# Row factors behind the second value pair, opening loads in pieces, and low parts on GpSimd, in a streaming hybrid layer on one core

## The chip, the core and the metric

The kernel runs on one core of a Trainium2 chip. A core has five engines that work side by side, each on its own queue of instructions, in order: TensorE (PE in the profile; PEld is its weight load) for matrix products, VectorE (DVE) and ScalarE (ACT) for elementwise work, GpSimd (POOL) for some more of that, and SyncE (SP), which here only issues transfers. Data lie in DRAM, in the on-chip SBUF (128 partitions) and in PSUM, the banks that TensorE writes to. Engines wait for each other by semaphores. The metric is the device time of one execution, in microseconds (us); a lower one is better.

## What is computed

The reference is one layer of a streaming encoder for 512 prompt frames and 64 frames of a running stream (576 in all, 2048 channels, fp32). The part that matters here is its beginning:

```python
hn = rmsnorm(x, g_norm1)
proj = hn @ w_in
q, k, v, gb, gc, hc = jnp.split(proj, [...], axis=-1)
q = rmsnorm(q.reshape(B, T, N_HEADS, HEAD_DIM), g_q)
k = rmsnorm(k.reshape(B, T, N_HEADS, HEAD_DIM), g_k)
v = v.reshape(B, T, N_HEADS, HEAD_DIM)
...
x = x + mix @ w_out
h2 = rmsnorm(x, g_norm2)
x = x + (jax.nn.silu(h2 @ w_gate) * (h2 @ w_up)) @ w_down
```

Attention (stick breaking), a short gated convolution and the output norms stand between; the change touches none of them.

## The kernel before

Activations are held with channels on the partitions and the 576 frames along the row, in two halves of 288. A product in fp32 is made of three products in a shorter format: a tensor is split into a high part (a cast) and a low part (tensor minus high part), and high x high, low x high and high x low are summed in PSUM. `split` (L230) does this: the cast on ScalarE, the subtraction on VectorE. Larger products then use a seven-product scheme on 2x2 blocks, which needs sums of blocks of the activations (b11, b12, bod and the sums t12a, t34a) and of the weights.

The row factor of the first norm, 1/sqrt(mean of squares), is not put on x. It is applied to the results, as a row vector R1 copied to all partitions.

The first 80 us of the kernel are one stage (L618 to L752). Its order on ScalarE, VectorE and SyncE is written by hand (`manual_schedule`), TensorE's is for the whole kernel; GpSimd's, and that of all engines but TensorE behind the stage, is left to the framework. It has two loops over the 16 blocks of 128 input channels (kt):

- The first loop turns x and computes the first value pair (heads 0 and 1). `turn_x(kt)` (L541) transposes a block of x on TensorE (four transposes for the prompt, and every fourth block four small ones for the sample frames), copies it out on ScalarE (st), scales it by the norm's gains g1c and splits it: the even blocks give b11 and b12 with the high part on ScalarE, the odd ones give bod, both parts on VectorE. `step0(0, ..., kt)` (L661) makes the 12 products of a block, LAG = 3 turns later. `split_wv` (L630) splits a quarter of the pair's weights, 1024 columns, into whi and wlo. Behind the loop the result goes to the tiles E0.
- The second loop computes the second value pair (heads 2 and 3) from the same blocks, `step0(1, ..., kt)`. Beside it ScalarE and VectorE sum the squares of x (`x_squares`, L604: three rows on ScalarE, the fourth on VectorE) and make the block sums for what follows: `x_sums(j)` (L573) computes, for a pair j of blocks, two scaled copies on ScalarE (b11s, b22s), t1 and t3 on VectorE, t2 = b22s - t1 on GpSimd and t4, which needs t2, on VectorE; `x_parts(j)` (L591) splits them into t12a and t34a. Pairs 0 to 2 are done in the first loop, 3 to 7 in the second.

In turn 9 of the second loop the squares are reduced, GpSimd takes the power (L730), VectorE puts the factors on the diagonal of `dg` (L737, turn 11), and in turn 13 TensorE transposes a block of vectors (`turn_vectors`) and multiplies `dg` by ones into PSUM (L743), from which VectorE copies R1. So turns 13 to 15 of the second pair stand behind these products in TensorE's queue.

Behind the stage the second pair is scaled by R1 (e1, L899), the first as well (e0, L904, on VectorE); `tokens` turns and stores them a number of TensorE's steps later. Then units of the projection follow in the list `order`: `run(n, p)` makes the p-th of seven products of a unit, `prepare(n, p)` splits its weights four places ahead; two of these splits, of the first unit, stand in the second loop already.

Loads and stores are issued by SyncE. The opening order (L636 to L653) is x, sample rows, gains, x, the first quarter of the value weights in one piece, x, and so on.

Of the kernel before, what the change touches and what calls it, by code (L numbers as in the profile page):

```python
# [16 lines left out]
P = 128  # L17
# [84 lines left out]
def tile_hybrid_stream_step(  # L102
# [405 lines left out]
    t12a, t34a = {}, {}  # L508

# [31 lines left out]
    def turn_x(kt):  # L541
        j, q = divmod(kt, 2)
        c = next(c for c, (k0, k1) in enumerate(XCH) if k0 <= kt < k1)
        k = kt - XCH[c][0]
        if kt % 8 == 0:
            banks["s"] = misc("psx_s")
# [4 lines left out]
        psx = ps_z.tile([P, 512], F32, tag=f"z{kt % 2}", name=f"psx{kt}")  # L551
        for i in range(4):
            nc.tensor.transpose(psx[:, i * P : (i + 1) * P], xin[c][:, i, k * P : (k + 1) * P], ident)
# [19 lines left out]
    def x_sums(j, tag):  # L573
# [7 lines left out]
        ta, tb = (tmp.tile([P, 2, HALF], F32, tag=tag, name="tab", bufs=3 if tag == "hl" else 2) for _ in range(2))  # L581
# [4 lines left out]
        nc.vector.scalar_tensor_tensor(out=t4, in0=od[:, :HALF], scalar=go, in1=t2, op0=ALU.mult, op1=ALU.subtract)  # L586
        tabs[j] = ta, tb

    tabs = {}

    def x_parts(j):  # L591
        ta, tb = tabs.pop(j)
# [25 lines left out]
    LAG = 3  # L618
    with tc.manual_schedule(engines={mybir.EngineType.Activation, mybir.EngineType.DVE, mybir.EngineType.SP}):
# [5 lines left out]
        def load_wv(v, q):  # L625
            c0 = 2 * AW + 2 * v * P
            nc.sync.dma_start(out=raw0(q).rearrange("p (k c) -> p k c", k=4),
                              in_=w_in[4 * q * P : 4 * (q + 1) * P, c0 : c0 + 2 * P].rearrange("(k p) c -> p k c", p=P))

        def split_wv(v, q):  # L630
            if q % 2 == 0:
                wv[v, q // 2] = [wpool.tile([P, 2048], F32R, tag=tag, name=tag) for tag in ("whi", "wlo")]
            hi, lo = (t[:, q % 2 * 1024 : (q % 2 + 1) * 1024] for t in wv[v, q // 2])
            split(hi, lo, raw0(q))

        load_x(0)  # L636
        load_s(0)
        nc.sync.dma_start(out=g1raw, in_=g_norm1[0].rearrange("(r c) -> r c", c=P))
        load_x(1)
        load_wv(0, 0)  # L640
# [32 lines left out]
        for kt in range(KD + LAG):  # L673
            if kt < KD:
                if kt == 0:
                    psg = misc("ps_g1")
                    nc.tensor.transpose(psg[:, :KD], g1raw, ident[:KD, :KD])
                    nc.vector.tensor_copy(out=g1c, in_=psg[:, :KD])
                turn_x(kt)
            if kt in (0, 4, 8, 12):  # L680
# [13 lines left out]
            if kt in (13, 15):  # L694
# [911 lines left out]
```

## Time and profile before

| | us |
|---|---|
| median of three runs | 2406.14 (2406.02 to 2406.74) |
| the profiled execution, its own time | 2408.49 |
| its span in the profile | 2406.8 |
| first value pair, from its first product to the second pair's | 12.13 to 46.05 |
| second value pair, up to the first product of the first unit | 46.05 to 80.31 |

The profile is of one execution. A row of a timeline gives the start, the duration, the engine, the line of the kernel, the operation, the tile written and the tiles read, the shape and the number of instructions; in brackets stands how long the engine had been idle before and what ended that. A row of the stretches gives for each engine the busy time and the number of instructions (PE, PEld, DVE, ACT, POOL), then the clock granted to TensorE (1.00 is full speed), the share of the transfer engines and GB/s. Consecutive rows of one engine can overlap slightly: what an instruction costs its queue is the distance from its start to the next one's.

### The profile page before, as it was taken

The page shows a single profiled execution, that of the slowest core. Times are in us where ns is not written, and L with a number is a line of the kernel's source. Part 1 is how long each engine was busy: PE and PEld are TensorE (multiplying, and loading weights), DVE is VectorE, ACT ScalarE, POOL GpSimd, SP SyncE. Part 2 cuts the span into 40 slices and gives each one's busy share as a digit, 9 for nine tenths or more (in the row PEclk, how much of TensorE's full clock was granted, in tenths as well). Part 3 has the DMA queues.
Part 4 walks back from the last instruction along what each step waited for, and adds up shares of the span by engine and source line. Part 5 has one row for each costly group of instructions (what it writes and reads, how often), then busy time and mean ns, then how long its engine had stood idle before and what let it go on. Part 6 is the DMA issues. An engine that isn't in the chain of part 4 may idle for free.

```text
span 2406.8 us, 43812 instructions
## 1 busy us (share of the span) xinstructions
PE 2355.5 (98%) x17609; PEld 2339.5 (97%) x17609; DVE 1939.7 (81%) x2840; ACT 1235.0 (51%) x2207; POOL 298.9 (12%) x377
## 2 busy tenths in 40 slices
PE   8899999999999999999999999999999899999998
PEld 8899999998889999999999999999999899999998
DVE  7888898797677768888888888888888778887875
ACT  7456656455677545444444444444444444444454
POOL 0111121120233222000000000000000002431211
PEclk9999999999999999999999999999999999999999
DMA  7433342535632233535444444444444936885642
GB/s 253 140 113 108 108 140 86 161 99 184 224 107 89 100 127 118 155 112 158 150 128 145 146 143 132 144 150 141 129 152 141 339 112 205 221 226 195 205 128 79
DMA packets 474900, 360.60 MB, mean 150 GB/s; under 512 B 11278, under 2 KB 460680, under 8 KB 474696
## 3 DMA queue, kind: packets, MB, share of 16 engines
q1 hardware_dynamic: 469528, 351.02, 45.7%
q0 software_dynamic: 5168, 6.79, 1.6%
q8 instruction: 138, 2.26, 0.4%
q14 instruction: 66, 0.54, 0.1%
HBM read 281.39 MB, written 76.37 MB: 149 GB/s over the span
## 4 chain that ended last, share of the span: by engine, by line
PE 82%; DVE 6%; ACT 4%; issue 2%; POOL 2%; DMA 1%; SPq 0%; ACTq 0%; DVEq 0%; POOLq 0%
PE psy L405 43%; PE psw L405 21%; PE psx L405 10%; PE pjo L227 5%; DVE whl L232 1%; ACT whl L231 1%; PE pw L1388 1%; ACT ph L231 0%; PE psv L405 0%; PE pot L1511 0%; DVE c L866 0%; DVE raw_b L349 0%; POOL hbl L1117 0%; DMA raw_a<-in_w_down_dram 0%; DVE wlo L180 0%
## 5 line engine op out<-in xcount | busy, mean ns | idle before, releaser
L232 DVE TENSOR_TENSOR whl<-raw_a,whl 128x1024 fp32r<-128x1024 f32 (+4 forms) x376 | 426.4, 1135 | 69.4 <-ACT whl L231 67.8
L405 PE MATMUL psy<-t,whl 128*128 128x288 f32 x2916 | 438.4, 295 | 0.5 <-ACT part L428 0.5
L231 ACT CAST whl<-raw_a 128x1024 fp32r<-128x1024 f32 (+4 forms) x376 | 352.6, 938 | 137.9 <-PE psx L405 47.8
L405 PE MATMUL psy<-h_s,whl 128*128 128x288 f32 x2724 | 411.7, 295 | 6.8 <-ACT part L428 6.8
L405 PEld LDWEIGHTS psy<-t,whl 128*128 128x128 f32 x2916 | 403.7, 189 | 0.9 <-ACT part L428 0.7
L405 PEld LDWEIGHTS psy<-h_s,whl 128*128 128x128 f32 x2724 | 378.5, 189 | 7.3 <-ACT part L428 7.3
L405 PE MATMUL psw<-t,whl 128*128 128x288 f32 x2592 | 377.1, 295 | 0.0
L405 PEld LDWEIGHTS psw<-t,whl 128*128 128x128 f32 x2592 | 354.4, 189 | 0.2
L232 DVE TENSOR_TENSOR whl<-raw_b,whl 128x1024 fp32r<-128x1024 f32 (+5 forms) x230 | 248.7, 1081 | 86.4 <-ACT whl L231 85.1
L231 ACT CAST whl<-raw_b 128x1024 fp32r<-128x1024 f32 (+5 forms) x230 | 207.6, 904 | 206.9 <-PE psw L405 70.8
L428 ACT COPY part<-psy 128x288 f32<-128x288 f32 x303 | 121.2, 400 | 348.5 <-PE psy L405 346.4
L405 PE MATMUL psx<-h_s,whl 128*128 128x288 f32 x1122 | 165.1, 295 | 2.7 <-DVE gs L1368 2.7
L405 PEld LDWEIGHTS psx<-h_s,whl 128*128 128x128 f32 x1122 | 154.1, 188 | 2.9 <-issue 2.9
L231 ACT CAST whl<-s 128x1024 fp32r<-128x1024 f32 (+5 forms) x101 | 93.4, 924 | 119.9 <-PE psw L405 112.3
L405 PE MATMUL psy<-t12a,whl 128*128 128x288 f32 x1056 | 150.5, 295 | 3.1 <-ACT part L428 3.1
L405 PE MATMUL psw<-t34a,whl 128*128 128x288 f32 x1056 | 150.4, 295 | 2.1 <-DVE ghs L854 0.9
L405 PEld LDWEIGHTS psy<-t12a,whl 128*128 128x128 f32 x1056 | 143.5, 188 | 4.0 <-ACT part L428 4.0
L405 PEld LDWEIGHTS psw<-t34a,whl 128*128 128x128 f32 x1056 | 143.2, 188 | 2.7 <-DVE ghs L854 1.1
L227 PE MATMUL pjo<-mixc,whi 128*128 128x288 f32 x512 | 123.0, 307 | 1.2 <-ACT kcT L1063 1.2
L232 DVE TENSOR_TENSOR whl<-s,whl 128x1024 fp32r<-128x1024 f32 (+5 forms) x101 | 107.5, 1064 | 19.6 <-ACT whl L231 18.0
L1331 POOL DMA_DIRECT2D hid_dram<-form x3 | 2.4, 809 | 921.1 <-DVE form L232 921.1
L227 PE MATMUL pjo<-mixa,whi 128*128 128x288 f32 x512 | 102.1, 295 | 0.0
(599 smaller groups left out, 4146.8 us busy)
## 6 DMA issues: line engine op xcount, KB each, us to landing
hid_dram<-form SPq DMA_DIRECT2D x147, 288.0 KB, 2.3
raw_a<-in_w_gate_dram SPq DMA_DIRECT2D x23, 1024.0 KB, 6.2
raw_a<-in_w_up_dram SPq DMA_DIRECT2D x23, 1024.0 KB, 5.5
raw_a<-in_w_in_dram SPq DMA_DIRECT2D x22, 1024.0 KB, 5.5
raw_b<-in_w_in_dram SPq DMA_DIRECT2D x22, 1024.0 KB, 7.9
raw_b<-in_w_gate_dram SPq DMA_DIRECT2D x21, 1024.0 KB, 6.6
raw_b<-in_w_up_dram SPq DMA_DIRECT2D x21, 1024.0 KB, 7.7
h_s<-hid_dram SPq DMA_DIRECT2D x10, 2016.0 KB, 9.2
```

The source lines that it names most:

```text
L227: mm(ps, w_[:, k, csl], x_[:, a:b], start=(k == 0 and n == 0), stop=(k == nk - 1 and n == 2))
L231: nc.scalar.copy(out=hi, in_=src)
L232: (lo_eng or nc.vector).tensor_tensor(out=lo, in0=src, in1=hi.bitcast(F32), op=ALU.subtract)
L405: mm(ps, whl[:, w_, j, :], x_, start=(start and j == 0 and q == 0), stop=(j == len(xs_) - 1 and q == 2), skip_group_check=True)
L428: nc.scalar.copy(out=t, in_=st["y"])
L1331: q.dma_start(out=hid_dram[fp][2 * n - 2 : 2 * n].rearrange("f p t -> p f t"), in_=t.bitcast(F32))
L1388: mm(pss[j, i], w_[:, k, j * P : (j + 1) * P], x_, start=(kk == 0 and k == 0 and n == 0), stop=(kk == 1 and k == 7 and n == 2))
```

## The change

It has these parts:

- `step0(0, ..., 0)` runs in turn 1, and LAG is 2 for the others. The block of x is transposed ahead of the sample rows and of the gains.
- The first quarter of the value weights is loaded and split in two halves; the first half is split by VectorE alone, at the head of its queue. The first sample rows and the gains are loaded by ScalarE's queue.
- The low parts of the four quarters of the second pair's weights are computed on GpSimd, the first two of them two turns earlier (turns 11 and 13 of the first loop), the others in turns 0 and 3 of the second loop. The scaling of e0 by R1 goes to GpSimd as well.
- t4 is moved from `x_sums` to the beginning of `x_parts` (`x_last`). In the second loop `x_parts(j - 1)` stands right behind `x_sums(j)`, and `x_parts(7)` behind the loop. The fourth row of squares of pairs 5 to 7 goes to ScalarE.
- The reduction of the squares moves to turn 11 and `dg` to turn 13; the products with ones, the copies of R1 and `turn_vectors` stand behind the 16 turns of the second pair. They use one full bank and part of a second, and the second pair's banks are z1, z2 and two shared ones in place of z0, z1 and two shared ones.
- The tokens of the value heads are turned some steps later.

```diff
-    def load_s(c):
+    def load_s(c, queue=nc.sync):
...
-        nc.sync.dma_start(out=xsn[c], in_=xs[:, 4 * c * P : 4 * (c + 1) * P])
+        queue.dma_start(out=xsn[c], in_=xs[:, 4 * c * P : 4 * (c + 1) * P])
...
-    def x_sums(j, tag):
+    def x_sums(j, tags):
...
         nc.vector.scalar_tensor_tensor(out=t1, in0=ev[:, HALF:], scalar=ge, in1=b11s, op0=ALU.mult, op1=ALU.subtract)
         nc.gpsimd.tensor_tensor(out=t2, in0=b22s, in1=t1, op=ALU.subtract)
         nc.vector.scalar_tensor_tensor(out=t3, in0=ev[:, HALF:], scalar=ge, in1=b22s, op0=ALU.mult, op1=ALU.subtract)
-        nc.vector.scalar_tensor_tensor(out=t4, in0=od[:, :HALF], scalar=go, in1=t2, op0=ALU.mult, op1=ALU.subtract)
         tabs[j] = ta, tb
+    def x_last(j):
+        (ta, tb), od, go = tabs[j], stp[j][:, 1], g1c[:, 2 * j + 1 : 2 * j + 2]
+        nc.vector.scalar_tensor_tensor(out=tb[:, 1], in0=od[:, :HALF], scalar=go, in1=ta[:, 1], op0=ALU.mult,
+                                       op1=ALU.subtract)
...
     def x_parts(j):
+        x_last(j)
         ta, tb = tabs.pop(j)
...
-    def x_squares(j):
+    def x_squares(j, eng=nc.scalar):
...
-                square(xin[c][:, i, :], ssx[:, i, c : c + 1], nc.vector if i == 3 else nc.scalar)
+                square(xin[c][:, i, :], ssx[:, i, c : c + 1], eng if i == 3 else nc.scalar)
...
-    LAG = 3
+    LAG = 2
...
+            if v == q == a == 0:
+                nc.vector.tensor_copy(hi, raw0(q)[:, a:b])
+                nc.vector.tensor_tensor(out=lo, in0=raw0(q)[:, a:b], in1=hi.bitcast(F32), op=ALU.subtract)
+            else:
+                split(hi, lo, raw0(q)[:, a:b], lo_eng)
...
         load_x(0)
-        load_s(0)
-        nc.sync.dma_start(out=g1raw, in_=g_norm1[0].rearrange("(r c) -> r c", c=P))
+        load_s(0, nc.scalar)
+        nc.scalar.dma_start(out=g1raw, in_=g_norm1[0].rearrange("(r c) -> r c", c=P))
+        load_wv(0, 0, 0, 2)
         load_x(1)
-        load_wv(0, 0)
+        load_wv(0, 0, 2, 4)
         load_x(2)
...
+                    split_wv(0, 0, 0, 2)
                 turn_x(kt)
-            if kt in (0, 4, 8, 12):
+                if kt == 1:
+                    split_wv(0, 0, 2, 4)
+                    step0(0, v0ps, 0)
+            if kt in (4, 8, 12):
                 split_wv(0, kt // 4)
...
-            if kt in (13, 15):
-                split_wv(1, (kt - 13) // 2)
+            if kt in (11, 13):
+                split_wv(1, (kt - 11) // 2, lo_eng=nc.gpsimd)
...
-            if kt >= LAG:
+            if LAG < kt:
                 step0(0, v0ps, kt - LAG)
...
-            if kt in (1, 4):
-                split_wv(1, 2 + kt // 4)
-            if kt in (0, 2, 4, 6, 8):
-                x_squares(3 + kt // 2)
+            if kt in (0, 3):
+                split_wv(1, 2 + kt // 3, lo_eng=nc.gpsimd)
+            if kt in (0, 2, 5, 8, 10):
+                j = {0: 3, 2: 4, 5: 5, 8: 6, 10: 7}[kt]
+                x_squares(j, nc.vector if j < 5 else nc.scalar)
...
-            if kt == 9:
+            if kt == 11:
                 nc.vector.reduce_sum(out=ssr, in_=ssx, axis=mybir.AxisListType.X)
...
-            if kt in (1, 4, 7, 10, 13):
-                x_sums(3 + (kt - 1) // 3, "hl")
+            if kt in (1, 4, 7, 9, 12):
+                j = {1: 3, 4: 4, 7: 5, 9: 6, 12: 7}[kt]
+                x_sums(j, ("hl", "hl" if j % 2 else "c1"))
+                if j > 3:
+                    x_parts(j - 1)
             if kt == 10:
                 prepare(-NA, 1)
-            if kt == 15:
+            if kt == 13:
+                dg = lpool.tile([P, UW - 2], F32, tag="c0", name="dg")[:, :T]
+                for i, (o, n) in enumerate(row_pieces()):
+                    nc.vector.tensor_scalar(out=dg[:n, o : o + n], in0=ident[:n, :n], scalar1=rst[:n, i : i + 1],
+                                            scalar2=None, op0=ALU.mult)
                 prepare(-NA, 2)
             step0(1, v1ps, kt)
+        psr, psv = (ps_pj.tile([P, 512], F32, tag="pj", name=name) for name in ("ps_r1", "ps_vec"))
+        for i, (o, n) in enumerate(row_pieces()):
+            mm(psr[:, o : o + n] if i < 4 else psv[:, P : P + n], oner.bitcast(F32)[:n, :], dg[:n, o : o + n],
+               start=True, stop=True)
+        nc.vector.tensor_copy(R1[:, :TP], psr)
+        nc.vector.tensor_copy(R1[:, TP:], psv[:, P : P + TS])
+        turn_vectors(psv)
...
-        pipe.spawn(tokens(e1[c], vp[:, 2 + c, :], vs[:, 2 + c, :], v_dram[2 + c], 4 + 5 * c))
+        pipe.spawn(tokens(e1[c], vp[:, 2 + c, :], vs[:, 2 + c, :], v_dram[2 + c], 9 + 5 * c))
...
-        nc.vector.tensor_tensor(out=e0[c], in0=e0[c], in1=R1, op=ALU.mult)
-        pipe.spawn(tokens(e0[c], vp[:, c, :], vs[:, c, :], v_dram[c], 24 + 8 * c))
+        nc.gpsimd.tensor_tensor(out=e0[c], in0=e0[c], in1=R1, op=ALU.mult)
+        pipe.spawn(tokens(e0[c], vp[:, c, :], vs[:, c, :], v_dram[c], 30 + 8 * c))
...
         prepare(*order[k_])
+    x_parts(7)
```

More of the change, by code (lines that the diff above doesn't have):

```diff
@@ L508, in tile_hybrid_stream_step @@
     t12a, t34a = {}, {}
+    UW = T + 4
     def a_frame(p_, j):
@@ L544, in turn_x @@
         k = kt - XCH[c][0]
+        psx = ps_z.tile([P, 512], F32, tag=f"z{kt % 2}", name=f"psx{kt}")
+        for i in range(4):
+            nc.tensor.transpose(psx[:, i * P : (i + 1) * P], xin[c][:, i, k * P : (k + 1) * P], ident)
         if kt % 8 == 0:
@@ L550, in turn_x @@
                 nc.tensor.transpose(banks["s"][:, o : o + TS], xsn[kt // 4][:, s * P : (s + 1) * P], ident[:TS, :TS])
-        psx = ps_z.tile([P, 512], F32, tag=f"z{kt % 2}", name=f"psx{kt}")
-        for i in range(4):
-            nc.tensor.transpose(psx[:, i * P : (i + 1) * P], xin[c][:, i, k * P : (k + 1) * P], ident)
+        if kt == 0:
+            psg = misc("ps_g1")
+            nc.tensor.transpose(psg[:, :KD], g1raw, ident[:KD, :KD])
+            nc.vector.tensor_copy(out=g1c, in_=psg[:, :KD])
         if q == 0:
```

46 lines of the change are left out of this document (15 added, 31 removed).

## The prediction, made before the changed kernel was run

> **What bounds the kernel now.** I read the page first, then the waits of TensorE, then the four engines in order of time over the first 120 us, because everything that the diff touches lies there.
>
> ```profile
> span 2406.8 us, 43812 instructions
> PE 2355.5 (98%) x17609; PEld 2339.5 (97%) x17609; DVE 1939.7 (81%) x2840; ACT 1235.0 (51%) x2207; POOL 298.9 (12%) x377
> ...
> PE ps_r L743 <- DVE dg L737: 5.1, 1, 5.1
> ...
> 72.00:80.30 8.30, 8.26 (x46) 7.92 (x47) 7.23 (x16) 2.31 (x3) 1.33 (x4) 0.73 0.36 107
> ```
>
> TensorE is busy for 98%: a microsecond gained or lost on it early on stays in the total, since what follows is matmuls back to back. The change can reach two holes: a wait for the second x block, and a 5.1 us wait for the scaled identity `dg`, after which the granted clock is low (0.73).
>
> ```profile
> 10.54 1.94 PE L553 MATMUL psx<-ident,xin 128*128 128x128 f32 x8 [2.87 <-DMA xin<-in_x_prompt_dram]
> ...
> 12.13 0.59 PE L670 MATMUL pj<-b,whi 128*128 128x288 f32 x1
> ...
> 15.19 0.47 PE L550 MATMUL psx_s<-ident,xsn 64*128 64x64 f32 x4
> ...
> 44.44 0.29 PE L670 MATMUL pj<-bod,whi 128*128 128x288 f32 x1
> ...
> 46.05 0.30 PE L670 MATMUL pjz<-b,whi 128*128 128x288 f32 x1
> ...
> 66.68 0.27 PE L261 MATMUL ps_vec<-ident,vecs 128*128 128x128 f32 x1
> ...
> 72.04 2.69 PE L743 MATMUL ps_r<-dg,oner 128*128 128x128 f32 x10 [5.09 <-DVE dg L737]
> ...
> 76.27 0.38 PE L670 MATMUL pjm<-bod,whi 128*128 128x288 f32 x1
> ...
> 80.31 1.88 PE L405 MATMUL psy<-b,whl 128*128 128x288 f32 x13
> ```
>
> The first value pair runs from 12.13 to 46.05, the second from there to 80.31, when the first unit (psy) starts. One step of 12 products takes (66.68 - 46.05) / 13 = 1.59 us. Who paces the first pair is seen on ScalarE:
>
> ```profile
> 20.37 0.59 ACT L557 COPY st<-psx 128x512 f32<-128x512 f32 x1 [1.06 <-PE psx L553]
> ...
> 28.49 0.69 ACT L231 CAST t12a<-tab 128x576 fp32r<-128x576 f32 x1
> 29.07 0.70 ACT L231 CAST t34a<-tab 128x576 fp32r<-128x576 f32 x1
> ...
> 41.43 0.60 ACT L557 COPY st<-psx 128x512 f32<-128x512 f32 x1
> ...
> 45.43 0.40 ACT L708 COPY E<-pj 128x288 f32<-128x288 f32 x1 [0.38 <-PE pj L670]
> ...
> 55.01 1.05 ACT L231 CAST whi<-raw_a 128x1024 fp32r<-128x1024 f32 x1
> 55.96 0.41 ACT L602 ACTIVATE xin<-xin 128x256 f32<-128x256 f32 x1
> ...
> 57.17 0.53 ACT L579 ACTIVATE b11s<-st,g1c 128x288 f32<-128x288 f32 x1
> 57.60 0.53 ACT L580 ACTIVATE b22s<-st,g1c 128x288 f32<-128x288 f32 x1
> ```
>
> From 20.37 to 45.04 ScalarE has no gap; its last copy of x is at 41.43, VectorE splits that, and TensorE takes it at 44.44. So the first pair is tight against ScalarE and VectorE, not only against TensorE. Start to start, a cast of 1024 columns costs 0.95 us there, one of 576 0.58, a row of squares 0.40, a scaled copy 0.43.
>
> **The change, part by part.**
>
> *Opening.* The load of the first weights is cut, and the first product step (3.06 us, 12.13 to 15.19) goes ahead of the wait for x. With the lag cut from 3 to 2, transpose 6 still has the same number of steps before it; it comes earlier only because the array is warm sooner. Its 12 products took 3.06 us, against 1.59 for a later step; with the wait filled, the steps from 10.54 on run at the later rate. I take 1.5 us, bounds 0 and 2.9 (the wait). The x block still lands at 10.5: the bytes ahead of it are the same. Rows against it:
>
> ```profile
> 0.80 1.28 ACT L119 ACT_TABLE_LOAD   x1 [0.80 <-PEq L1593]
> ...
> 1.96 0.57 SPq L638 DMA_DIRECT2D vecs<-in_g_norm_dram  x1
> ...
> 4.90 0.26 PE L677 MATMUL ps_g<-ident,vecs 16*128 16x16 f32 x1 [4.90 <-DMA vecs<-in_g_norm_dram]
> ...
> xin<-in_x_prompt_dram SPq DMA_DIRECT2D x2, 256.0 KB, 3.0
> ```
>
> On ScalarE's queue the gains are issued after the table load and the sample rows, near 2.7 in place of 1.96, and land near 5.7. The x transposes now stand ahead, so this is covered. VectorE first waits for the 256 KB piece of weights (issued near 1.3, landing 3.0 later), and `g1c` stands behind it; it is done near 6, as ScalarE ends its first copy. Cost 0: both hide under the wait up to 10.54, and some 0.8 us late would still do so.
>
> *GpSimd.* Four low parts (1024 columns) and two scalings of E (576) leave VectorE. What that is worth depends on these rows:
>
> ```profile
> 25.97 0.94 POOL L584 TENSOR_TENSOR tab<-b22s,tab 128x288 f32<-128x288 f32 x1 [24.59 <-DVE tab L583]
> ...
> 26.94 0.52 DVE L586 SCALAR_TENSOR_TENSOR tab<-st,g1c,tab 128x288 f32<-128x288 f32 x1 [0.70 <-POOL tab L584]
> ...
> 107.22 1.23 DVE L232 TENSOR_TENSOR whl<-raw_a,whl 128x1024 fp32r<-128x1024 f32 x1
> ...
> 107.30 1.81 POOL L844 TENSOR_TENSOR c<-c,R 128x288 f32<-128x288 f32 x1 [8.36 <-DVE c L843]
> ...
> 138.95 2.53 POOL L869 TENSOR_TENSOR c<-c,R 128x512 f32<-128x512 f32 x2 [8.04 <-DVE c L866]
> ...
> 139.09 2.23 DVE L232 TENSOR_TENSOR whl<-raw_a,whl 128x1024 fp32r<-128x1024 f32 x1
> ...
> L232 DVE TENSOR_TENSOR wlo<-raw_a,whi 128x1024 fp32r<-128x1024 f32 x8 | 9.8, 1222 | 1.4 <-ACT whi L231 1.3
> ```
>
> A split that takes 1.22 alone took 2.23 when GpSimd had begun 0.14 us before it: VectorE stood still until GpSimd's 512 columns were through, 138.95 to about 140.1. The other way round GpSimd waited: 288 columns, 0.94 otherwise, took 1.81 behind a split that was not lengthened. The two exclude each other. 1024 columns then keep VectorE out for 2 x 1.2 = 2.4 us, to save 1.14 (start to start). Bounds: 0 (GpSimd in VectorE's idle time, as after 107.22) and 1024 / 288 x 0.94 = 3.3. I take 2.4, from the widest row.
>
> [...]
>
> *t4 moved into `x_parts` (`x_last`).* Before, VectorE idled 0.70 us for GpSimd's t2 in most turns (the row at 26.94). Now it has work there, but work with two SBUF inputs, held up by the same t2: no gain. But ScalarE's second cast (t34a), ready at once in the rows 28.49 and 29.07, now waits for a t4 that stands further back in VectorE's queue. Steps there, start to start:
>
> ```profile
> 27.38 0.52 DVE L565 SCALAR_TENSOR_TENSOR b<-st,g1c,b 128x288 fp32r<-128x288 f32 x1
> ...
> 28.24 1.22 DVE L232 TENSOR_TENSOR wlo<-raw_a,whi 128x1024 fp32r<-128x1024 f32 x1
> 29.37 0.52 DVE L569 TENSOR_SCALAR bod<-st,g1c 128x576 fp32r<-128x576 f32 x1
> 29.92 0.82 DVE L570 SCALAR_TENSOR_TENSOR bod<-st,g1c,bod 128x576 fp32r<-128x576 f32 x1
> ```
>
> With the row at 26.94 that is 0.44 for t4, 1.13 for a low part, 0.55 for the first bod and, with 0.74 for the second (0.82 less the 0.08 by which such rows overlap), 1.29 for both.
>
> *First pair, summed on ScalarE.* Opening -1.5. The cast of the second pair's second quarter now stands before the last x copy: +0.95. `x_parts(0)`: behind the cast of weight quarter 2 ScalarE needs 0.47 + 0.58 to be ready, VectorE 1.13 + 1.29 + 0.44 and some 0.2 of handing over: +2.0. `x_parts(1)`: ScalarE is ready 0.47 + 0.95 + 0.58 = 2.0 after the cast of quarter 3. VectorE is 1.3 behind by then (t2 and the first GpSimd low part held it), and needs 1.13, the hold of 2.4, 1.29 and 0.44, 6.6 in all: +4.6. Sum +6.1: the last copy goes from 41.43 to about 47.5. Its 0.6 and the two bod follow, to 49.4; ten of the last 12 products need the second of them (10 x 0.133), so the pair ends near 50.8 in place of 46.05: **+4.8**.
>
> *Second pair, to `dg`.* ScalarE's rows from there to the last cast ahead of `dg`: squares of six pairs (3 at 1.2, 3 at 1.6), six scaled pairs at 0.86, five pairs of casts at 1.17, three weight casts at 0.95, two E copies at 0.4: 23.1. Waits for t4, now behind the next pair's t1 and t3: 0.43 + 0.94 + 0.44, and less the 0.58 of the cast beside it, so 1.3 (rounded up for handing over) four times, and once 2.4 more, where GpSimd's last low part holds t1: 7.6. From 48.1 that gives 78.8; with the wait for the end of the first pair (0.4) and the last low parts on VectorE (1.1) `dg` starts near 80.3, in place of 71.70. `x_parts(7)` is out of that chain, t1 and t3 of pair 7 are in it.
>
> *Row factors behind the pair.* This is the gain: the last three steps no longer stand behind the wait. TensorE ends the pair at 50.8 + 16 x 1.59 = 76.2, waits to about 80.6, turns the factors in 2.69 (cold again: 4.4 us of idling; 5.09 did it before) and the vectors in 0.27, so psy starts near 83.6. In the rows 72.04 to 76.27 the low rate lasted 4.2 us: 1.1 us of it fall on psy, 0.5 lost. Net 84.1 - 80.31 = **+3.8**. Freed banks: no wait on them in the list, 0. [...]
>
> *After it.* VectorE's queue to the third product of the first unit:
>
> ```profile
> 74.16 0.69 DVE L744 COPY R<-ps_r 128x512 f32<-128x512 f32 x1 [1.04 <-PE ps_r L743]
> ...
> 89.91 2.96 DVE L232 TENSOR_TENSOR whl<-raw_a,whl 128x1024 fp32r<-128x1024 f32 x2
> ...
> 94.91 0.41 PE psv L405 x3
> ```
>
> Without contention the first of the pair at 89.91 would be ready at 91.1; TensorE took it at 94.91. After, the copies end near 84.3; the queue loses 3.9 (t1, t3, a split, two E) and gains 2.8 of holds by the two E on GpSimd, so it is ready near 99.4, and wanted at 84.1 + 14.6 = 98.7. Between 0 and 1.6, I take **+0.8**. Token lags only move transposes and stores; the fewer squares on VectorE for pairs 5 to 7 (3 x 0.43) are in the chain above as ScalarE's 1.6.
>
> Sum: 3.8 + 0.8 = +4.6 on the profiled execution's 2408.49, 2413.1; that execution stood 2.35 above the median of the runs, so 2406.14 + 4.6, rounded to **2411**.
>
> **Rivals.** (1) *VectorE is relieved as meant.* Place: the two stretches where GpSimd's low parts run. If they hold nobody, `dg` is ready by 72, the second pair ends near 72 too, there is no wait and no cold spell: factors and vectors at the warm rate, half of 2.69 + 0.27, psy at 73.4, -6.9: 2399. It decides as soon as `dg` is ready before the pair ends. For it: row 107.22, and that GpSimd's order is not written by hand, so that its low parts may be put elsewhere; against it: 139.09. (2) *Half of the holds fall into VectorE's waits.* Two of four, 4.8 us off the chain: `dg` at 75.5, no cold spell, psy near 77.5, -2.8: 2403. For it: VectorE waits for ScalarE in the second pair. (3) *Wide GpSimd work is slower,* 3.3 each by the narrow row: 0.9 more four times, and 0.5 for each E by the same row, +4.5: 2415. It decides if the wlo rows on GpSimd are over 3 us with VectorE out of the way.
>
> **How the numbers follow.** Forecast 0.52, own range 2408 to 2415; rivals 0.22, 0.14 and 0.12. About 0.2% (4.8 us) is what a measurement of this kernel can tell from no change, so its edges are 2401.3 and 2410.95. The forecast's costs reach further up (3.3 for a hold) than down, so I put 0.30 of it above the upper edge; with rival 3, slower is 0.42. Faster: rival 1 and 0.04 of rival 2, 0.26. Within: the rest, 0.32. The range holds the forecast and reaches to rivals 1 and 3 at both ends, 2399 to 2416.
>
> **What would show it.** First pair ending after 49, with t34a casts that wait for t4; VectorE splits of over 2 us beside GpSimd's wlo; `dg` near 80 and a wait of about 4 us at the row factors. I am wrong if wlo on GpSimd lengthens nothing, or if psy starts before 78.

## The result, and the profile after

The changed kernel took 2416.72 us (median of six runs, 2414.34 to 2418.47) beside 2406.63 for the kernel before on the same chip: 1.0042 times as long, 95% interval 1.0031 to 1.0053, or **10.1 us slower**. The forecast was 4.9 us slower, its range ended 0.7 us below the result. The profiled execution took 2416.04, 7.5 more than that of before: it is a short one for the changed kernel, as that of before was a long one.

The page after, and two rows of TensorE's waits (engine, line and what it waited for: us in all, times, the longest):

```profile
span 2414.3 us, 43820 instructions
PE 2359.9 (98%) x17609; PEld 2341.4 (97%) x17609; DVE 1942.6 (80%) x2830; ACT 1234.3 (51%) x2213; POOL 311.9 (13%) x383
...
PE psy L405 <- ACT part L428: 11.7, 8, 6.3
PE ps_r L768 <- DVE dg L762: 4.7, 1, 4.7
```

The same 17609 products kept TensorE busy for 2359.9 us, 4.4 more than before: over half of the 7.5 is not waiting, but the same work at a lower rate.

TensorE's timeline after, from the end of the second pair on:

```profile
76.34 0.29 PE L689 MATMUL pjz<-bod,whi 128*128 128x288 f32 x1
81.34 2.08 PE L768 MATMUL ps_r<-dg,oner 128*128 128x128 f32 x8 [4.71 <-DVE dg L762]
...
84.35 0.47 PE L261 MATMUL ps_vec<-ident,vecs 128*128 128x128 f32 x1 [0.32 <-DVE R L771]
84.48 4.73 PE L405 MATMUL psy<-b,whl 128*128 128x288 f32 x24
89.05 0.95 PE L405 MATMUL psx<-bod,whl 128*128 128x288 f32 x6
...
108.61 3.47 PE L405 MATMUL psy<-t12a,whl 128*128 128x288 f32 x24 [1.17 <-ACT part L428]
```

The wait for `dg` is nearly as long as before (4.71 for 5.09), only the whole pair stands ahead of it now. Behind it the 24 products of the first unit take 4.57 us (84.48 to 89.05); in the second pair of before, at a granted clock of 1.00, products behind each other take 0.133 each (a step of 12 takes 1.59), 3.2 for 24. The first unit's second product (psx, 89.05) started 5.1 us later than before (83.95), although before had the first token transposes ahead of it, and at the last row TensorE waits 1.17 for a copy on ScalarE where it waited 0.49.

The first loop and the second, on GpSimd, VectorE and ScalarE:

```profile
34.73 2.62 POOL L232 TENSOR_TENSOR wlo<-raw_a,whi 128x1024 fp32r<-128x1024 f32 x1 [8.52 <-ACT whi L231]
...
35.02 2.61 DVE L612 SCALAR_TENSOR_TENSOR xin<-xin 128x256 f32<-128x256 f32 x1
...
40.64 2.62 POOL L232 TENSOR_TENSOR wlo<-raw_a,whi 128x1024 fp32r<-128x1024 f32 x1 [1.49 <-ACT whi L231]
...
40.96 2.63 DVE L574 TENSOR_SCALAR bod<-st,g1c 128x576 fp32r<-128x576 f32 x1
...
44.90 0.68 ACT L231 CAST t34a<-tab 128x576 fp32r<-128x576 f32 x1 [3.76 <-DVE tab L597]
...
58.05 2.41 POOL L232 TENSOR_TENSOR wlo<-raw_a,whi 128x1024 fp32r<-128x1024 f32 x1 [0.34 <-ACT whi L231]
...
58.45 2.33 DVE L590 SCALAR_TENSOR_TENSOR tab<-st,g1c,b11s 128x288 f32<-128x288 f32 x1 [0.44 <-ACT b11s L584]
...
76.50 1.41 POOL L751 TENSOR_TENSOR vecs<-vecs 128x5 f32<-128x5 f32 x1 [5.23 <-DVE vecs L750]
77.90 1.12 POOL L591 TENSOR_TENSOR tab<-b22s,tab 128x288 f32<-128x288 f32 x1
...
79.06 0.67 ACT L231 CAST t12a<-tab 128x576 fp32r<-128x576 f32 x1 [2.77 <-POOL tab L591]
...
79.06 0.52 DVE L597 SCALAR_TENSOR_TENSOR tab<-st,g1c,tab 128x288 f32<-128x288 f32 x1 [0.68 <-POOL tab L591]
80.33 0.76 DVE L232 TENSOR_TENSOR t34a<-tab,t34a 128x576 fp32r<-128x576 f32 x1 [0.76 <-ACT t34a L231]
81.01 1.03 DVE L762 TENSOR_SCALAR dg<-ident,vecs 128x128 f32<-128x128 f32 x5
```

A square of 256 columns, 0.42 us elsewhere, takes 2.61; the first bod, 0.52 elsewhere, 2.63: VectorE stands still until GpSimd is through (at 37.35 and 43.26 by the rows; the square ends at 37.63, the bod at 43.59). ScalarE waits 3.76 us for t4 at its second cast. `dg` comes at 81.01. Ahead of it, by the count of the eight pairs' rows, stand rows of pair 7: GpSimd computes t2 (77.90) only behind the power (76.50), ScalarE's cast of t12a waits 2.77 us for it, and VectorE's t4 (79.06) 0.68. The code has that cast and that t4 behind the loop, in `x_parts(7)`; here they run ahead of pair 6's t34a, whose low part (80.33) `dg` follows.

Where the time was lost between the stage and the end is seen in the clock granted to TensorE. The stretches were cut where it changes; it is 0.50 or 1.00, nothing between. Before, and after:

```profile
69.62:76.45 6.83, 4.41 (x17) 4.07 (x18) 5.76 (x15) 1.31 (x3) 1.26 (x4) 0.50 0.82 248
```

```profile
80.54:87.37 6.83, 5.71 (x23) 5.30 (x24) 6.34 (x16) 3.17 (x4) 2.99 (x4) 0.50 0.02 6
87.37:110.00 22.63, 21.46 (x164) 21.22 (x163) 21.60 (x22) 10.30 (x17) 5.39 (x4) 1.00 0.51 158
```

TensorE worked 4.41 us of the slow stretch before, 5.71 of it after. Counted by the clock of 0.50, half of such work is lost, an estimate: 2.2 us before, 2.9 after. The 8 row factor products took 2.08 us there, and 1.16 at 1.00 (after_warm, at 81.31).

### The profile page after: what moved, and what is told of

Read it like the earlier page. It is cut to its first block, busy times and chain, and to the rows that moved or that the text cites. A ratio compares the mean times of both kernels' runs of the same rounds, so it can differ in the third digit from the quotient of the medians.

```text
span 2414.3 us, 43820 instructions
## 1 busy us (share of the span) xinstructions
PE 2359.9 (98%) x17609; PEld 2341.4 (97%) x17609; DVE 1942.6 (80%) x2830; ACT 1234.3 (51%) x2213; POOL 311.9 (13%) x383
## 3 DMA queue, kind: packets, MB, share of 16 engines
q1 hardware_dynamic: 469432, 350.88, 45.5%
## 4 chain that ended last, share of the span: by engine, by line
PE 82%; DVE 7%; ACT 5%; issue 2%; POOL 2%; DMA 1%; SPq 0%; ACTq 0%; DVEq 0%; POOLq 0%
PE psy L405 43%; PE psw L405 21%; PE psx L405 10%; PE pjo L227 5%; DVE whl L232 1%; ACT whl L231 1%; PE pw L1408 1%; ACT ph L231 0%; DVE raw_b L349 0%; PE pot L1531 0%; DVE c L885 0%; ACT xin L614 0%; POOL hbl L1137 0%; DMA raw_a<-in_w_down_dram 0%; DVE wlo L180 0%
```

## The experiments

All ratios are to the kernel before, from runs on the same chip, where its medians were 2407.45 to 2408.16 (2406.63 for the first row). Each kernel is the changed one but for the edit that is shown, and all compute the whole layer. The last column lists the slow stretches between 64 and 124 us, cut where the granted clock changes. Seven of the profiles have one of 3.41 or 6.83 us in the first pair too, between 38 and 47 us; the second pair starts no later in them than in the changed kernel's first profile, which has none there. One of ten executions of lo_t4 took 5917.06 us, which does not move its median.

| run | median, us | ratio, 95% interval | wait for `dg` | slow stretches, us |
|---|---|---|---|---|
| the changed kernel | 2416.72 | 1.0042 (1.0031 to 1.0053) | 4.71 | 6.83 |
| after_again | 2416.74 | 1.0039 (1.0025 to 1.0053) | 4.71 | 10.24, 3.41 |
| lo_vec | 2412.10 | 1.0018 (1.0008 to 1.0027) | 3.61 | 10.24 |
| t4_back | 2411.48 | 1.0019 (1.0010 to 1.0028) | 0.68 | 6.82 |
| lo_t4 | 2404.81 | 0.9988 (0.9978 to 0.9998) | none | 3.41 |
| lo_t4_e0 | 2403.96 | 0.9986 (0.9976 to 0.9995) | none | 3.41 |
| after_turn | 2412.74 | 1.0020 (1.0011 to 1.0029) | 5.51 | 6.82 |
| after_warm | 2418.21 | 1.0043 (1.0026 to 1.0060) | 0.25 | 10.24 |
| turn_warm | 2413.65 | 1.0028 (1.0016 to 1.0040) | 1.06 | 3.41 |
| lo_t4_turn | 2401.82 | 0.9977 (0.9968 to 0.9987) | none | none |
| after_lag | 2414.33 | 1.0032 (1.0021 to 1.0044) | 4.72 | 10.24, 3.41 |
| turn_e0_lag | 2403.33 | 0.9981 (0.9971 to 0.9990) | none | none |
| before_again | 2407.69 | 1.0002 (0.9993 to 1.0011) | 5.11 | 6.83 |
| after_tok | 2416.55 | 1.0034 (1.0021 to 1.0047) | 4.71 | 10.24, 3.42 |
| after_e0 | 2413.05 | 1.0025 (1.0015 to 1.0034) | 4.71 | 10.24 |
| lo_t4_turn_tok | 2407.33 | 0.9995 (0.9985 to 1.0004) | none | 3.41 |

### The same kernels again

**after_again**, no edit.

> The changed kernel once more, for a second profile of it. If the extra time is the two VectorE chains alone, the span is within 1 us of 2414.3 and the first unit starts near 84.5 us again. If the length of the cold spell behind the 4.7 us wait differs from one execution to the next, the start of the second unit's product (89.05 in the first profile) moves by 1 us or more and the mean granted clock with it.

The first unit started 0.4 us earlier (84.06), its second product 0.9 us later (89.91), just under the 1 us named: the spread lies between these two and behind them, not in the stage. The stretches of this execution:

```profile
79.58:89.82 10.24, 8.57 (x35) 8.17 (x36) 9.41 (x19) 3.72 (x5) 5.06 (x5) 0.50 0.02 6
89.82:110.31 20.49, 18.59 (x143) 18.35 (x142) 17.44 (x18) 9.48 (x17) 3.32 (x2) 1.00 0.56 171
110.31:113.72 3.41, 3.41 (x14) 3.41 (x15) 2.06 (x2) 0.83 (x1) 0.00 (x0) 0.50 0.10 30
```

The slow stretch is 10.24 us long, and a second one follows a wait of 1.91 us for the copy of part. Half of 8.57 + 3.41 is 6.0 us lost, against 2.9 in the first profile of the same program.

**before_again**, no edit.

> The kernel before once more, for a second profile of it. Theory (the profile of before is a fair one, and its wait of 5.09 us for dg with the slow products behind it is always there): median within 0.1% of the other runs of before, the second pair starts at 45.5 to 47 us, the wait for dg is 4.8 to 5.4 us, and the first unit starts within 1 us of 80.31. Rival (the profiled execution shown was a long one, by 1.9 us over its median, through its opening): the second pair starts below 45.5 us.

The wait for `dg` was 5.11 us, the first unit started at 79.64, 0.67 earlier than in the first profile. The second pair started at 45.44, just below the rival's 45.5: the profile that the forecast was made on was a little long there.

### The parts of the change on GpSimd and VectorE

**lo_vec**: the low parts of the second pair's weights back on VectorE (two places like this one, four low parts).

```diff
-                split_wv(1, (kt - 11) // 2, lo_eng=nc.gpsimd)
+                split_wv(1, (kt - 11) // 2)
```

> The changed kernel with the four low parts of the second pair's weights back on VectorE, at the same places. Theory (GpSimd and VectorE exclude each other, so each low part on GpSimd costs VectorE 2.4 us in place of 1.14): dg starts near 76.5 in place of 81.0, the first unit near 80, about 4 us less than the changed kernel. Rival (GpSimd's work is off the path and only the place of t4 matters): no change, within 1 us. Rival (VectorE really is relieved): 4 us more.

4.6 us less on the median, as the theory had it, but not by its steps: `dg` came at 78.29, 2.7 us earlier and not 4.5, the first unit at 81.76 and not near 80, with a slow stretch of 10.24 us beside it. What makes up the rest of the 4.6 is not shown: at the first product of psw this profile stands 1.9 us ahead of the changed kernel's first and 5.1 ahead of its second. No row is held by a low part any more: in its VectorE timeline the square stands as

```profile
36.17 0.42 DVE L612 SCALAR_TENSOR_TENSOR xin<-xin 128x256 f32<-128x256 f32 x1
```

**t4_back**: t4 in the sums again, as before.

```diff
         tabs[j] = ta, tb
+        x_last(j)
...
     def x_parts(j):
-        x_last(j)
```

> The changed kernel with t4 computed in x_sums again, the low parts still on GpSimd. Theory (ScalarE's second cast waits for a t4 that stands too far back in VectorE's queue, 3 to 4 us in the first pair and 1.0 to 2.8 four times in the second): dg starts near 77, the first unit near 79.5, about 5 us less than the changed kernel. Rival (the low parts alone make the loss): VectorE idles for t2 again, no change or 2 us more.

5.2 us less: `dg` comes at 75.21, 5.8 us earlier, and the wait for it falls to 0.68. But a wait of 3.56 us for the copies of R1 took its place: in TensorE's timeline

```profile
80.63 0.48 PE L261 MATMUL ps_vec<-ident,vecs 128*128 128x128 f32 x1 [3.56 <-DVE R L771]
80.76 5.63 PE L405 MATMUL psy<-b,whl 128*128 128x288 f32 x24
```

**lo_t4**: both edits.

> The changed kernel with both undone: low parts on VectorE, t4 in x_sums. Theory: the two costs add up, dg starts near 70 and is ready before the second pair ends, TensorE doesn't wait at the row factors and stays warm, the first unit starts near 72.5: about 8 us less than before, 2398. Rival (the opening or the moved row factors are a loss by themselves): not faster than before, 2406 or more.

No wait for `dg` is left (it comes at 70.74), as expected, yet only 3.0 us are won against the kernel before, not 8, and the first unit starts at 76.25, not 72.5. On VectorE and TensorE stand, in the order of time,

```profile
74.17 1.21 DVE L347 TENSOR_TENSOR s<-raw_b 128x1024 f32<-128x1024 f32 x1
75.30 0.68 DVE L770 COPY R<-ps_r 128x512 f32<-128x512 f32 x1
75.90 0.21 DVE L771 COPY R<-ps_vec 128x64 f32<-128x64 f32 x1
...
76.17 0.33 PE L261 MATMUL ps_vec<-ident,vecs 128*128 128x128 f32 x1 [2.93 <-DVE R L771]
76.25 4.94 PE L405 MATMUL psy<-b,whl 128*128 128x288 f32 x24
```

The turn of the vectors writes into the bank that holds the last 64 columns of the row factors, so it waits for their copy, and VectorE, which is early now, splits t12a and t34a and sums weights ahead of it. The wait of 2.93 us brings a slow stretch (77.39 to 80.80) with it.

**lo_t4_e0** and **after_e0**: the scaling of E0 back on VectorE, on top of lo_t4 and by itself.

```diff
-        nc.gpsimd.tensor_tensor(out=e0[c], in0=e0[c], in1=R1, op=ALU.mult)
+        nc.vector.tensor_tensor(out=e0[c], in0=e0[c], in1=R1, op=ALU.mult)
```

> The changed kernel with the low parts back on VectorE, t4 back in the sums, and the scaling of E0 back on VectorE: of the three jobs that the change gives to GpSimd or moves, none is left; what stays is the opening and the row factors behind the pair. Theory (the scaling on GpSimd is hidden): within 0.7 us of the same kernel with the scaling on GpSimd, which took 2404.8. Rival (it holds VectorE, whose two splits at 77.89 took 3.33 in place of 2.34): 1 to 2 us shorter, about 2403.

0.85 us less, within what two medians of this kind can tell apart.

> The changed kernel with the scaling of E0 back on VectorE, and nothing else. Theory (hidden, as the sum had it: without the other GpSimd parts this edit moved the median by 0.85 us): within 1 us of the changed kernel's 2416.7, with the dg wait of about 4.7 us as it is. Rival (the scaling holds VectorE by 0.8 us in its two splits and so delays the weights' sums, the loads behind them and the token stores): the wait for part is 0.5 us and the whole 2 us or more shorter.

3.7 us less: the rival by its time, though the wait for part was 0.87 and not 0.5. Its mechanism is not borne out: counted from the first row factor product, VectorE is through its two splits 8.5 us later, and 8.0 in the changed kernel (the splits took 2.35 in place of 3.17, but 1.42 of scaling stand ahead of them). The second slow stretch is gone; why the scaling on GpSimd cost 3.7 us here and 0.85 on top of lo_t4 stays open.

### The wait for the copies of R1

**after_turn**: the turn of the vectors moved into the second pair, in a bank of its own.

```diff
             if kt == 13:
+                turn_vectors(ps_pj.tile([P, 512], F32, tag="pj", name="ps_tv"))
                 dg = lpool.tile([P, UW - 2], F32, tag="c0", name="dg")[:, :T]
...
-        turn_vectors(psv)
```

> The changed kernel with one thing moved: the turn of the vectors stands inside the second pair (k-tile 13), in a bank of its own, and not behind the copies of R1. Theory (the wait that this order adds is small while dg is late, 0.32 us in the changed kernel's profile, since VectorE has nothing else to do ahead of the copies): the first unit's product starts 0.4 to 0.6 us earlier after the row factors' products, and the whole is 0.3 to 1.0 us shorter than the changed kernel. Rival (the order itself is what costs): TensorE's clock comes back sooner as well, the first 24 products take 3.2 us and not 4.6 to 6.0, and the whole is 2 us or more shorter.

4.0 us less: the rival. The 24 products still took 4.35 us (83.81 to 88.16), so not all of its picture held. But the slow stretch is 6.82 us long where four other profiles with that wait and the late `dg` show 10.24 (after_again, after_lag, after_tok, after_e0), as lo_vec does with a wait of 3.61; no second stretch follows, and the 0.32 us is gone:

```profile
79.40:86.22 6.82, 5.03 (x20) 4.69 (x21) 6.53 (x17) 3.23 (x4) 3.10 (x5) 0.50 0.02 5
86.22:120.00 33.78, 31.94 (x239) 31.24 (x239) 28.99 (x31) 13.85 (x21) 7.03 (x5) 1.00 0.55 168
```

**lo_t4_turn**: lo_t4 with the same edit.

> The changed kernel with the low parts of the second pair's weights back on VectorE, t4 back in the sums, and the turn of the vectors inside the second pair in a bank of its own, so that TensorE does not wait for the copies of R1. Without the last edit the first unit's product started at 76.25 us and its 24 products took 4.94 us. Theory (that wait of 2.93 us and the slow rate behind it are what is left of the change's cost): the first unit starts at 73.0 to 73.5, its 24 products take 3.2 to 3.5 us, and the whole is 3 to 4.5 us shorter than without the edit, about 2401. Rival (the next operand is as late: VectorE splits the next two units' weights after the copies): TensorE waits 1 to 2 us for whl at about 80, and the whole is 1 to 2 us shorter, about 2403.

The theory: 3.0 us less than lo_t4, the lower end of what was expected, with the first unit at 71.96, 24 products in 3.28, and the clock at 1.00 throughout.

```profile
66.00:100.00 34.00, 31.44 (x234) 30.41 (x233) 30.24 (x41) 14.62 (x24) 11.47 (x9) 1.00 0.57 171
```

At 2401.82 us it is 0.23% **faster than the kernel before** (interval 0.13 to 0.32%), and the best of the versions that ran.

### Work in the place of the wait

**after_warm**: 34 products ahead of the row factors; **turn_warm**: the same with the moved turn.

```diff
+        psd = ps_pj.tile([P, HALF], F32, tag="pj", name="ps_d")
+        for i in range(34):
+            mm(psd, wv[1, 1][0][:, :P], bod[:, 7, 0, 0, :], start=True, stop=True)
         psr, psv = (ps_pj.tile([P, 512], F32, tag="pj", name=name) for name in ("ps_r1", "ps_vec"))
```

> The changed kernel with 34 products more, of 288 columns, into a bank that nobody reads, between the second pair and the row factors' products: TensorE works through most of its wait for dg (4.5 of 4.7 us). It leaves nothing out. Theory (the wait is paid a second time, by a slow rate behind it): the wait shrinks below 0.5 us, the 8 row factor products take about 1.05 us in place of 2.08, the first 24 products of the first unit 3.2 to 3.5 in place of 4.7 to 6.0, and the whole is 2.5 to 4 us shorter than the changed kernel. Rival (the slow products come from ports or memory, as GpSimd and the tokens work at that time): the 24 products take 4.5 us or more all the same and the whole moves by less than 1 us.

The 8 row factor products took 1.16 us in place of 2.08, as the theory has it. But the framework then put VectorE's splits and sums ahead of the copies of R1, and the gain was lost in a new wait:

```profile
81.31 1.16 PE L771 MATMUL ps_r<-dg,oner 128*128 128x128 f32 x8 [0.25 <-DVE dg L762]
82.40 0.43 PE L771 MATMUL ps_vec<-dg,oner 64*128 64x64 f32 x2
88.79 0.47 PE L261 MATMUL ps_vec<-ident,vecs 128*128 128x128 f32 x1 [5.96 <-DVE R L774]
```

> The changed kernel with two edits together: the turn of the vectors inside the second pair in a bank of its own, and 34 products more into a bank that nobody reads in TensorE's wait for dg. It differs from the kernel with the moved turn alone by these products only; there the 8 row factor products took 2.08 us, the 24 behind them 4.51, psx began at 88.16 us, and the median was 2412.74. Theory (work behind a long wait runs at a slow rate and costs about 2 us here): 1.1 to 1.2 us for the 8, 3.2 to 3.5 for the 24, psx at 86.0 to 86.7, and a median of 2410.5 to 2411.5. Rival (the slow rate has another cause, or the gain is taken back by the waits of the first units): psx moves, but the second product of t12a moves by less than 0.7 us and the median stays above 2412.

All three rates came out as the theory said (1.16, 3.28, psx at 86.29). From the first row factor product to psx it took 4.73 us, and 6.97 without the 34 products (81.19 to 88.16): slow work behind the wait costs 2.2 us here. The whole did not gain: E1, whose scaling stands behind the same late copies, was not there, TensorE waited 1.86 us at 89.10, and a new slow stretch of 3.41 us began at 90.18.

### The wait for part in the first units

**after_lag**: the tokens' due times of before; **turn_e0_lag**: the same on top of lo_t4_turn and of the scaling of E0 on VectorE.

```diff
-..., v_dram[2 + c], 9 + 5 * c))
+..., v_dram[2 + c], 4 + 5 * c))
...
-..., v_dram[c], 30 + 8 * c))
+..., v_dram[c], 24 + 8 * c))
```

> The changed kernel with the tokens' due times of before: 4 and 9 for E1, 24 and 32 for E0, in place of 9 and 14, 30 and 38. Theory (the later tokens of E0 put ScalarE's last token copy, which waits for a store of the tokens to leave its buffer, ahead of the copy of part that TensorE waits for): the wait for part behind the first product of t12a falls from 1.17 and 1.91 us in the two profiles to 0.5, no slow products follow it, and the whole is 0.7 to 3 us shorter than the changed kernel, 2413.7 to 2416. Rival (E0, scaled on GpSimd at 84.4 to 87.1 us, or E1 is not there at the earlier due times, or the tokens' copies hold ScalarE elsewhere): TensorE waits for E or another part copy and the whole is the same or longer, 2416.5 or more.

Inconclusive. The median is 2.4 us lower, but the mechanism is not there: the wait for part was 2.33 us and slow products followed.

> The changed kernel with the low parts, t4 and the scaling of E0 back as before, the turn of the vectors inside the second pair in a bank of its own, and the tokens' due times of before: only the opening and the row factors behind the pair are left of the change. The same with the scaling on GpSimd and the later due times took 2401.82, with a wait of 1.71 us for part behind the first product of t12a. Theory (that wait comes from the late tokens): 0.5 us there, and a median of 2400.3 to 2401.3. Rival (the wait comes from ScalarE's other work, since all of it stands earlier now): 1.5 us or more there and a median of 2401.5 to 2403.

The wait for part fell from 1.71 to 0.77, but TensorE waited 1.45 us for E at 77.48 instead, and the whole is 1.5 us longer: the theory's time is missed. Whether the earlier due times or the scaling of E0 on VectorE made E late, this run does not tell.

**after_tok**: the small token copies in two other tiles, so that none waits for a store.

```diff
-        tb = hl_tile("tokz")[:, :P]
+        tb = (tmp.tile([P, HALF], F32, tag=ztag, name="tokz", bufs=1) if ztag else hl_tile("tokz"))[:, :P]
...
```

`ztag` is "ms" for c = 0 and "t" for c = 1.

> The changed kernel with other buffers for the small token copies (the last 64 rows' copies of E1 and E0), so that they no longer wait for a store of tokens to leave one of three shared buffers. Theory (late stores, bunched with the weights' loads that start late after the pause, hold ScalarE and through it the copy of part that TensorE waits for): no token copy waits for a store of v between 95 and 112 us, the wait for part behind the first product of t12a is 0.5 us in place of 1.17, 1.91 and 2.33 us, the 24 products behind it take 3.4 to 3.5 us, and the whole is 1 to 3 us shorter than the changed kernel's 2416.7. Rival (the copy of part is late because of ScalarE's weight casts, which are late with their loads): the wait stays above 1 us and the whole within 1 us.

The rival: the same time, and the wait for part 1.87 us. ScalarE in the changed kernel and in this one:

```profile
107.05 0.27 ACT L789 COPY tokz<-tok_b 128x128 f32<-128x128 f32 x1 [1.74 <-DMA v_dram<-tok]
107.21 1.05 ACT L231 CAST whl<-raw_a 128x1024 fp32r<-128x1024 f32 x1
108.16 0.40 ACT L428 COPY part<-psy 128x288 f32<-128x288 f32 x1
```

```profile
106.70 1.05 ACT L231 CAST whl<-raw_a 128x1024 fp32r<-128x1024 f32 x1 [1.30 <-DVE raw_a L353]
107.66 1.04 ACT L231 CAST whl<-raw_b 128x1024 fp32r<-128x1024 f32 x1
108.81 0.40 ACT L428 COPY part<-psy 128x288 f32<-128x288 f32 x1
```

Without the wait for the store ScalarE waits for a sum on VectorE (L353) at the cast behind it. Two holds of about the same length stand behind each other; taking one away shows the other.

**lo_t4_turn_tok**: the same on top of lo_t4_turn.

> The changed kernel with the low parts on VectorE, t4 back in the sums, the turn of the vectors inside the second pair in a bank of its own, and other buffers for the small token copies. Without the last edit it took 2401.82, with a wait of 1.71 us for part behind the first product of t12a. Theory (that wait comes from the stores): 0.5 us there, 2400.3 to 2401.0. Rival (casts): 1.5 us or more there, 2401.5 or more.

Not a test of either: the two tiles taken are those of part itself, whose copy now waited 1.48 us for a token store, TensorE 4.00 us for the copy, and the time rose by 5.5 us. In after_tok no such wait shows. What the stores alone cost stays open.

## Why the prediction came out too small

**What held.** The direction did, and the two costs behind it. GpSimd's low parts took 2.41 to 2.62 us (forecast 2.4) and held VectorE for 2.2, 2.1 and 1.8 us in three rows and for 0.7 in the fourth (55.44, 1.18 for 0.52); lo_vec puts their price at 2.7 us at `dg` and 4.6 in all. The held rows read one tensor (40.96, 2.63 us for 0.52) or two (58.45, 2.33 for 0.52), and GpSimd's short t2 holds too, as forecast: beside it t4 took 1.05, 1.06 and 1.07 us (61.12, 65.83, 70.53) and 0.51 elsewhere (44.36). Not every row is held: two copies out of PSUM beside t2 (50.70, behind 50.49) took 0.81, as in before (48.02). The waits for t4 were 1.95 and 3.76 us in the first pair and 2.81, 1.00 and 1.01 in the second (forecast 2.0 and 4.6, then 7.6 in five); t4_back puts their price at 5.8 us at `dg` and 5.2 in all. Rival 1, in which `dg` comes before the pair ends, appears only once both parts are undone (lo_t4).

**What came out by luck.** The second pair started at 51.08 (forecast 50.8), `dg` at 81.01 (80.3), TensorE waited 4.71 (4.4). Behind the first two of these stand errors that cancel. At the first t34a cast ScalarE was, its wait aside, 0.6 us earlier than before and not the 1.5 put down for the opening; the second wait for t4 was 0.8 us shorter than forecast. In the second pair the waits for t4 came to 4.8 us and not 7.6, but `x_parts(7)`, which the prediction took out of the chain, was in it: ScalarE's wait of 2.77 us for pair 7's t2 makes up the difference, and `dg` came some 1.9 us later for it by the rows (80.33 could have followed 77.62 at once). No run tests that alone. And eight profiles that share these first 51 us started the second pair at 49.4 to 51.1, so that 0.3 us is less than executions differ by.

**Opening.** TensorE no longer waits for the second x block (2.87 us before), and its second step, 1.67 us long, starts at 12.69 (1.71 at 16.00 before; the first took 3.12 and 3.06), but by the end of the first pair nothing of it is left: with lo_t4's family the second pair starts at 44.9 to 46.7, in the two profiles of before at 45.4 and 46.05.

**The step that failed** is the end of "Row factors behind the pair": "the low rate lasted 4.2 us: 1.1 us of it fall on psy, 0.5 lost", with the turn of the vectors priced at its 0.27 us and no wait for the copies of R1 ahead of it. The rate does not come back a fixed time after work begins: it was 4.4 us in before (72.04 to 76.45), 6.0 and 8.9 in the changed kernel's two executions (81.34 to 87.37, 80.93 to 89.82). All slow stretches of the table are 3.41, 6.83 or 10.24 us long, one, two or three times the same length, and in the changed kernel's profile they lie on one grid: the first begins at 80.54 and the next at 609.60, 529.06 us or 155 times 3.413 later. So what counts, by these rows, is where the wait and the small gaps behind it fall on this grid. The new gap of 0.32 us is what after_turn took away: 6.82 us of slow stretch then, 10.24 in four of the five profiles that have the gap and the late `dg`, and in lo_vec, and 4.0 us on the median. In the first profile of the changed kernel the gap stands at a point of the grid (84.03 for 83.95), and 6.83 us were enough; in the others it stands 0.57 us or more from one. That the place decides is read from these few profiles, not shown by an experiment.

From the first row factor product to the second product of the first unit the changed kernel's two executions took 7.7 and 9.0 us (81.34 to 89.05, 80.93 to 89.91). The forecast had 0.5 us for the slow rate on the unit; it lost 1.4 (4.57 for 3.2) and 2.7 (5.85). That the slow rate behind the wait is the cause is shown by turn_warm: with work in the place of the wait the same way took 4.73 us, and 6.97 without that work (after_turn).

**"After it", +0.8,** was mis-sized as well, and put in the wrong place. The weights for the third product were in time; the wait grew at the copy of part: 1.17 and 1.91 us for 0.49, and where it passed 1.8 a slow stretch of 3.41 us followed, another 1.7 us by the clock of 0.50. From the second product of the first unit to the start of psw before took 25.66 us in both its profiles, the changed kernel 26.84 and 29.11: 1.2 and 3.4 more, of which some 0.4 are token transposes of E1 that stood ahead of that point before. So 0.8 and 3.0 are left: in the first profile the size is the forecast's, by luck, since the wait is another.

**Not in the sum: the attention.** It has waits of its own (over 0.4 us, from 604 on: 0.59, 1.71, 0.68 and 2.63 us in the changed kernel; from 602 on in after_turn, the kernel with the moved turn: 0.60, 1.71, 0.68, 0.47 and 1.99), and slow stretches beside them that differ. In the 30 us behind 614 the changed kernel has

```profile
614.00:624.00 10.00, 10.00 (x69) 9.77 (x69) 5.16 (x12) 5.04 (x10) 0.87 (x2) 0.88 1.03 355
624.00:634.00 10.00, 7.22 (x52) 6.73 (x51) 6.21 (x16) 6.65 (x16) 2.15 (x4) 0.98 0.98 321
634.00:644.00 10.00, 10.00 (x64) 9.91 (x64) 8.04 (x18) 7.58 (x16) 2.55 (x7) 0.85 0.44 170
```

and the kernel with the moved turn, in the same place of its work,

```profile
612.00:622.00 10.00, 10.00 (x77) 9.84 (x77) 5.74 (x12) 5.22 (x12) 1.34 (x3) 1.00 1.01 352
622.00:632.00 10.00, 7.40 (x54) 6.71 (x53) 6.36 (x16) 7.29 (x18) 2.54 (x6) 1.00 1.00 333
632.00:642.00 10.00, 9.48 (x63) 8.78 (x62) 7.66 (x17) 7.34 (x17) 2.46 (x5) 1.00 0.55 198
```

From the first product of pjo (598.13 us in before, 604.33 in the changed kernel) to the first of pw behind the attention (901.35 and 908.59) the changed kernel took 1.0 us longer than before, its second execution 0.8; after_turn took 1.2 less, and the second profile of before the same. On the way the two profiles of before stand up to 1.4 us apart and come level again. Whether what is left follows from when the stage ends or is chance stays open.

**The sum.** Against the profiled execution 4.6 were forecast and 7.5 measured, step by step: 5.1 at the second product of the first unit (forecast 3.8), 6.3 at psw (4.6), 7.5 at the end. The rest of the median's 10.1 is the two executions: before's was 1.9 over its median in that comparison, the changed kernel's 0.7 under its own, with a slow stretch of 6.83 us and no second one where after_again had 10.24 and 3.41. Between the second profiles, after_again and before_again, 6.6 us are lost at the second product of the first unit and 10.1 at psw, of 10.9 at the end: the stage and the first units are nearly the whole loss. The undos of the low parts, t4 and the turn (4.6, 5.2 and 4.0 us) add up to 13.8; lo_t4_turn, which has all three, is 14.9 faster than the changed kernel. Without them the rest of the change is a gain over before.

## What to carry to other kernels

In the stage and the first units a wait of TensorE of 1.86 us or more was paid twice, the second time in one to three lengths of 3.41 us at a granted clock of 0.50: price it by the work that falls into them, and look for small gaps behind it (6.82 us in after_turn, without the gap of 0.32 us, and 10.24 in four of five profiles with it). Before work moves to GpSimd, list what VectorE would run beside it: here four low parts saved VectorE 1.1 us each and held it for up to 2.2. When an edit makes an engine early, look at what the framework then puts ahead of the row on the path; a small product should not share a bank with a result whose copy can wait (2.93 us in lo_t4, 3.56 in t4_back, 5.96 in after_warm).

## What had not been expected

- The low clock came behind waits shorter than one such length of 3.41 us: 1.86, 1.87 and 1.91 us of idling (turn_warm, after_tok, after_again) were each followed by one stretch of 3.41 us, and 1.17, 1.45 and 1.71 were not (after, turn_e0_lag, lo_t4_turn). Further back the length of the wait does not decide alone: behind 1.71 us in the attention (609.36 in the changed kernel) a slow stretch began at 609.60, and behind 2.68 at 972.43 the clock stayed at 1.00.
- The same program gives 2.9 or 6.0 us of lost work in two executions, though its waits for `dg` were 4.71 us in both. The rows differ in where the slow stretch begins (80.54 for a wait that ended at 81.34, 79.58 for one at 80.93) and, behind that, in the wait for part (1.17 and 1.91); that the first brought the second is not shown.
